# Feed-forward up projections of two transformer blocks: all 16 slabs make two products first, and five products each in a second pass

## The chip, the cores and the metric

The kernel runs on one core of a Trainium2 chip. Its time is the device time of one execution in microseconds (us), as the median of the executions shown. The profile is of one execution, which has its own time and its own span (first to last instruction). PE is the engine of matrix products, DVE and POOL are the two that add and subtract whole tiles, ACT copies, casts and applies Relu and Square, SP only issues DMAs. ACT and POOL issue DMAs as well. Each engine has its own list of instructions and runs it strictly in order; between engines they wait on semaphores.

## The reference, cut to what matters

Two transformer blocks follow each other on one sequence of 1024 tokens of width 1024, in float32. Each ends in a feed-forward layer with a hidden width of 4096:

```
h = rms_norm(x, ffn_pre_norm)
f = square(relu(h @ w_up)) @ w_down
x = x + rms_norm(f, ffn_post_norm)

h2 = modulate(rms_norm_2(x, g_pre_mlp), sh2, sc2)
ff = square(relu(h2 @ w_mlp_in)) @ w_mlp_out
x  = x + gt2 * rms_norm_2(ff, g_post_mlp)
```

The change lies in `h @ w_up` and `h2 @ w_mlp_in`. The second block also needs `mod = c @ w_ada + b_ada`, six rows of 1024; the first two are made beside the first block's up projection.

## The kernel before, in words

Every float32 operand is split in two parts (hi and lo), and a product is three matmuls: hi by hi, hi by lo, lo by hi (`mm3`, L169). The up projection saves multiplications by a scheme of Strassen's kind: tokens and the width of the model are halved, so that `h` has four quarters, and instead of eight quarter products a slab of 256 hidden columns takes seven, on sums of quarters. A product has 12 matmuls of 128 by 512 columns (four steps of the width, three matmuls each), so a slab of seven has 84, and one stage with 16 slabs has 1344. The four quarters of the first half of the tokens (`b11` and `b21`, hi and lo) are the tiles `hq`, those for the other five products (`b22`, `t1` to `t4`) the tiles `hq_t`.

The stage (`up_stage`) runs twice, once in each block. First the output projection of the attention goes over two halves of the tokens. The epilogue of the second half (norm, transposes, `hq_t`) takes long, so PE is given other work meanwhile: the two products of 12 slabs that need `hq` alone (`LEAD`, L1032 and L1141 to L1151). Weights for it come a pair of slabs at a time through `load_w`, with one raw buffer `w_raw` and two buffers each of `w_hi` and `w_lo`. Their results are copied out of PSUM by ACT (L1150) into one of two staging tiles with one buffer each, and stored to `fx_dr` by a DMA on ACT (L1151). Then `slab` (L1060) goes over all 16 slabs: it loads the whole 256 columns of weights again (L1065; raw buffers `w_raw` and `fraw` in turn), DVE makes four sums of weight quarters in `fws` (L1073), ACT casts each part to hi (L1079) and copies it to PSUM (L1081), DVE subtracts for lo (L1082). The first two parts lie in one pair of `w_hi` and `w_lo`, the other three in the second pair, so a slab takes all the buffers there are. PE makes five products for slabs 0 to 11 (loading the two stored ones back, L1098) and seven for slabs 12 to 15. Each product has one of six PSUM buffers. DVE adds the products up (L1105 to L1132), in tiles `fx`, `fu2`, `fu3`, `f11`, `f00`; ACT applies Relu and Square (L1050, L1051). Last, POOL makes five more sums of the four results for the down projection (L1137) in tiles `fs` and stores each by a DMA of its own (L1043); ACT stores the other two. `fu2`, `fu3`, `f11` and `fws` have one buffer each, `fs` two.

In block 1, `side(c)` adds a step of `modulation` after each slab: DVE multiplies rows of `w_ada` by a column (L1245, L1247) out of 512 KB tiles.

Which instruction stands where in each engine's list is set by a scheduler at build time from its own estimates; `tc.high_priority` lets the lead products go ahead. After the stage, `ffn_down` begins with weights that POOL subtracts (L1180).

Of the kernel before, what the change touches and what calls it, by code (L numbers as in the profile page):

```python
# [65 lines left out]
def tile_two_blocks(ctx: ExitStack, tc: tile.TileContext, I, out):  # L66
# [965 lines left out]
    LEAD = 12  # L1032

    def lead_w(w_up, c):

        return load_w([w_up[:, 256 * (c + i):256 * (c + i) + P].rearrange("(k p) n -> p k n", p=P) for i in range(2)],
                      16, P)

    def ffn_up(hq, w_up, fl, fp, first, side):
# [13 lines left out]
        def p1(pool, a11):  # L1053
            acc = mm_tile()
            product(acc, a11, "b11")
            x = pool.tile([P, 512], F32, name="fx")
            ACT.copy(x, acc)
            return x

        def slab(c, lead):  # L1060
# [16 lines left out]
            def halves_of(t, n, v):  # L1077

                ACT.copy(t[0][:, n], v)  # L1079
                pt = tr_tile().rearrange("p (k n) -> p k n", k=4)  # L1080
                ACT.copy(pt, r32(t[0][:, n]))  # L1081
                DVE.tensor_tensor(out=t[1][:, n], in0=v, in1=pt, op=ALU.subtract)  # L1082

            def op(t, n):
                return [x[:, n] for x in t]
# [4 lines left out]
            halves_of(u[0], 0, s2)  # L1090
            halves_of(u[0], 1, s3)
            halves_of(u[1], 0, s1)
            halves_of(u[1], 2, a22)
            halves_of(u[1], 1, s4)
            if lead:
                x, f11 = (fp.tile([P, 512], F32, name=nm) for nm in ("fx", "f00"))
                for i, t in enumerate((x, f11)):
                    SP.dma_start(t, fx_dr[:, 512 * (2 * c + i):512 * (2 * c + i) + 512])  # L1098
                q2 = f11
            else:  # L1100
# [5 lines left out]
            if not lead:
                q2 = mm_tile()
                product(q2, op(u[0], 3), "b21")
                f11 = fp.tile([P, 512], F32, name="f00")
# [542 lines left out]
```

## Time and profile before

| | us |
|---|---|
| median of 3 executions (lowest, highest) | 2893.92 (2881.35, 2893.98) |
| the profiled execution | 2892.09 |
| its span | 2890.4 |
| PE busy in the span | 2659.9 (92%) |
| DVE, ACT, POOL busy | 1898.6, 1404.9, 833.3 |

The profiled execution's own time is 1.7 us more than its span, which is what lies around the program. Busy times of PE hide short pauses and a slow clock, because matmuls overlap in the pipeline; a stage is read from the starts of its first and last matmul, and from the row that says what each pause waited for. The granted clock of PE stands as a share of its full speed: 1.00 is 2.4 GHz and 0.5 is 1.2 GHz.

### The profile page before, as it was taken

The numbers are of one execution on the slowest core, as the hardware profiler recorded it, in microseconds if no ns is written. First come the engines' busy times: TensorE is split into PE (matmuls) and PEld (weight loads), VectorE is DVE, ScalarE is ACT, GpSimd is POOL, SyncE is SP. The second block draws the span as 40 slices with busy tenths as digits, with TensorE's granted clock in tenths as the row PEclk, the third lists the DMA queues.
The fourth block names the chain that finished last, engine by engine and source line by source line (L and its number), as shares of the span: only waits on it lengthen the run. The fifth ranks groups of instructions, "written<-read, shape, count | busy, mean of one in ns | idle before, by whom it ended". The sixth has DMA issues, their size and how long they took to land.

```text
span 2890.4 us, 39700 instructions
## 1 busy us (share of the span) xinstructions
PE 2659.9 (92%) x13801; PEld 2242.6 (78%) x13801; DVE 1898.6 (66%) x3526; ACT 1404.9 (49%) x2608; POOL 833.3 (29%) x840
## 2 busy tenths in 40 slices
PE   8999999999777889999999999989999778989996
PEld 7788889998656668877887788877897666778785
DVE  7668799768656655577745368785477555545665
ACT  4544666455545644354511256563278445543342
POOL 1242344200244451434100022112200444552413
PEclk9999999999898999999999999999999898999998
DMA  3386585357556467777654554436656454387785
GB/s 127 94 286 195 157 235 159 109 170 246 188 192 207 155 245 244 269 255 250 212 180 164 189 166 139 121 106 204 211 183 227 159 175 160 139 296 240 257 282 191
DMA packets 377406, 562.24 MB, mean 195 GB/s; under 512 B 39427, under 2 KB 215658, under 8 KB 377206
## 3 DMA queue, kind: packets, MB, share of 16 engines
q1 hardware_dynamic: 348278, 488.39, 52.3%
q0 software_dynamic: 12800, 41.95, 3.6%
q10 hardware_dynamic: 16128, 29.37, 2.7%
q8 instruction: 109, 1.79, 0.3%
q14 instruction: 91, 0.75, 0.1%
HBM read 408.83 MB, written 150.78 MB: 194 GB/s over the span
## 4 chain that ended last, share of the span: by engine, by line
PE 22%; DMA 13%; DVE 8%; ACT 5%; POOL 4%; issue 4%; SPq 0%; POOLq 0%; ACTq 0%; DVEq 0%
PE mm L173 19%; DMA dwr<-in_w_mlp_out 3%; DMA fs<-fs 3%; DVE w_lo L179 2%; POOL fs L1137 2%; POOL dwr L1180 1%; PE po L906 1%; DVE w_lo L209 1%; PE tr L898 1%; ACT w_hi L178 1%; DMA w_raw<-in_w_mlp_out 1%; DMA mixR<-mrg 1%; POOL w_raw L1180 1%; DMA m_sg<-sig 1%; ACT w_hi L203 1%
## 5 line engine op out<-in xcount | busy, mean ns | idle before, releaser
L173 PE MATMUL mm<-w_hi,df 128*128 128x512 f32 x1792 | 560.6, 393 | 20.8 <-ACT w_hi L178 13.5
L173 PE MATMUL mm<-hq_t,w_hi 128*128 128x512 f32 x1280 | 415.9, 408 | 114.1 <-DVE fu L1105 103.2
L173 PEld LDWEIGHTS mm<-w_hi,df 128*128 128x128 f32 x1792 | 338.9, 189 | 96.6 <-ACT w_hi L178 14.8
L173 PEld LDWEIGHTS mm<-hq_t,w_hi 128*128 128x128 f32 x1280 | 251.5, 198 | 179.0 <-DVE fu L1105 65.4
L173 PE MATMUL mm<-w_lo,df 128*128 128x512 f32 x896 | 352.7, 394 | 10.0 <-DVE w_lo L179 9.9
L173 PE MATMUL mm<-h_hi,w_hi 128*128 128x512 f32 x736 | 290.9, 395 | 0.0
L173 PE MATMUL mm<-h_lo,w_hi 128*128 128x512 f32 x736 | 289.4, 393 | 0.0
L173 PE MATMUL mm<-h_hi,w_lo 128*128 128x512 f32 x736 | 289.0, 393 | 0.0
L173 PE MATMUL mm<-hq_t,w_lo 128*128 128x512 f32 x640 | 256.6, 404 | 1.4 <-DVE w_lo L1082 1.4
L209 DVE TENSOR_TENSOR w_lo<-w_raw,w_hi 128x1024 fp32r<-128x1024 f32 (+1 forms) x138 | 172.8, 1276 | 101.6 <-ACT w_hi L203 101.1
L203 ACT CAST w_hi<-w_raw 128x1024 fp32r<-128x1024 f32 (+1 forms) x138 | 138.8, 1048 | 165.2 <-PE mm L173 57.6
L179 DVE TENSOR_TENSOR df<-dfr,df 128x1024 fp32r<-128x1024 f32 x112 | 160.3, 1445 | 87.1 <-ACT df L178 86.9
L173 PEld LDWEIGHTS mm<-w_lo,df 128*128 128x128 f32 x896 | 169.7, 189 | 49.9 <-DVE w_lo L179 15.4
L1180 POOL TENSOR_TENSOR dwr<-dwr 128x1024 f32<-128x1024 f32 x40 | 99.5, 2488 | 317.7 <-DMA dwr<-in_w_mlp_out 183.9
L173 PE MATMUL mm<-w_hi,mixT 128*128 128x256 f32 x1024 | 184.9, 282 | 5.8 <-DVE m_sg L1448 2.8
L1137 POOL TENSOR_TENSOR fs<-f,f 128x512 f32<-128x512 f32 x32 | 43.9, 1372 | 469.1 <-ACT f L1051 459.7
L1082 DVE TENSOR_TENSOR w_lo<-fws,tr 128x512 fp32r<-128x512 f32 x128 | 85.6, 685 | 140.5 <-ACT tr L1081 139.6
L179 DVE TENSOR_TENSOR w_lo<-dwr,w_hi 128x1024 fp32r<-128x1024 f32 x56 | 104.6, 1869 | 101.4 <-ACT w_hi L178 101.0
L178 ACT CAST df<-dfr 128x1024 fp32r<-128x1024 f32 x112 | 115.6, 1050 | 108.8 <-PE mm L173 75.6
L173 PEld LDWEIGHTS mm<-h_hi,w_hi 128*128 128x128 f32 x736 | 138.3, 188 | 33.8 <-issue 2.8
L173 PEld LDWEIGHTS mm<-w_hi,mixT 128*128 128x128 f32 x1024 | 157.6, 189 | 7.8 <-ACT w_hi L203 5.1
L1137 POOL TENSOR_TENSOR fs<-fu,f 128x512 f32<-128x512 f32 x96 | 129.6, 1352 | 114.0 <-DMA fs<-fs 110.3
(418 smaller groups left out, 6306.8 us busy)
## 6 DMA issues: line engine op xcount, KB each, us to landing
dfr<-fs SPq DMA_DIRECT2D x112, 512.0 KB, 6.3
fs<-fs POOLq DMA_DIRECT2D x160, 256.0 KB, 2.6
w_raw<-in_w_in SPq DMA_DIRECT2D x32, 1024.0 KB, 4.9
ada_raw<-in_w_ada SPq DMA_DIRECT2D x48, 512.0 KB, 4.3
w_raw<-in_w_down SPq DMA_DIRECT2D x48, 512.0 KB, 4.1
dwr<-in_w_down SPq DMA_DIRECT2D x48, 512.0 KB, 5.4
w_raw<-in_w_mlp_out SPq DMA_DIRECT2D x48, 512.0 KB, 6.2
dwr<-in_w_mlp_out SPq DMA_DIRECT2D x48, 512.0 KB, 4.6
```

What stands on the lines that cost most here:

```text
L173: PE.matmul(ps, l, r, start=first and n == 0, stop=final and n == last)
L178: ACT.copy(hi, src)
L179: DVE.tensor_tensor(out=lo, in0=src, in1=r32(hi), op=ALU.subtract)
L203: ins = ACT.copy(wh[:, step * i:step * i + step], raw[:, step * i:step * i + step])
L209: DVE.tensor_tensor(out=wl[:, c], in0=raw[:, c], in1=r32(wh[:, c]), op=ALU.subtract)
L898: PE.transpose(pt[:, 256 * j + P * i:256 * j + P * i + P], prob[i][:, ks], ident)
L906: PE.matmul(po[:, d:], vb if j else va, t[:, 256 * j:256 * j + 256 - d], start=n == 0 and m == 0, stop=n == len(groups) - 1 and m == 3)
L1082: DVE.tensor_tensor(out=t[1][:, n], in0=v, in1=pt, op=ALU.subtract)
L1137: POOL.tensor_tensor(out=t, in0=x, in1=z, op=o)
L1180: POOL.tensor_tensor(out=a, in0=a, in1=b, op=ALU.subtract if sub else ALU.add)
```

## The change

All 16 slabs go through the first pass (two products each), and the second loop makes five products for every slab; the seven-product form is gone. So `fx_dr` holds 16 slabs instead of 12. Since nothing reads `hq` after the first pass, its four tiles get new uses: `hq0` is the raw buffer of odd slabs (in place of `fraw`), `hq1` and `hq2` hold the weight sums in turn (in place of the one `fws`, which slab 0 still uses), and `hq3` takes the rows of `w_ada`, 1 MB a load instead of 512 KB, with the next load issued ahead. With the space saved, `fu2`, `fu3` and `f11` get two buffers each and `fs` seven.

```diff
-    "fp": "fws fraw fx*2 f00*2 fu2 fu3 f11 fs*2 ada_acc ada_raw*2",
+    "fp": "fws fx*2 f00*2 fu2*2 fu3*2 f11*2 fs*7 ada_acc",
...
-    fx_dr = scratch("fx_dr", (P, 2 * 12 * 512))
+    fx_dr = scratch("fx_dr", (P, 2 * 16 * 512))
...
+            self.b = [[self.tile(2 * g + i, [P, 4, 512], F32R) for i in range(2)] for g in range(2)]
+        def tile(self, i, shape, dtype):
+            return self.pool.tile(shape, dtype, name=f"hq{i}")
...
+        with tc.high_priority(offset=100):
+            for c in range(NC):
+                if c % 2 == 0:
+                    w = first if c == 0 else even_w(w_up, c)
+                for i, b in enumerate(("b11", "b21")):
+                    acc = product([t[:, 8 * (c % 2) + 4 * i:8 * (c % 2) + 4 * i + 4] for t in w], b)
+                    x = fl.tile([P, 512], F32, name=("fx", "f00")[i])
+                    ACT.copy(x, acc)
+                    ACT.dma_start(fx_dr[:, 512 * (2 * c + i):512 * (2 * c + i) + 512], x)
+        for c in range(NC):
             if c % 2:
-                raw = fp.tile([P, 2048], F32, name="fraw")
+                raw = hq.tile(0, [P, 2048], F32)
...
-            ws = fp.tile([P, 4, 4, P], F32, name="fws")
+            ws = fp.tile([P, 4, 4, P], F32, name="fws") if c == 0 else hq.tile(1 + c % 2, [P, 4, 4, P], F32)
...
-            if not lead:
-                halves_of(u[0], 2, a11)
-                halves_of(u[0], 3, a12)
...
-                x = p1(fp, op(u[0], 2))
...
+            w6, w7, w5, w4, w3 = [parts(*a) for a in ((0, 0, s2), (0, 1, s3), (1, 0, s1), (1, 1, a22), (1, 2, s4))]
...
-        for c in range(LEAD):
...
-        for c in range(NC):
-            slab(c, c < LEAD)
...
-                g = modulation(fp, 0, 2)
+                g = modulation(fp, 0, 2, lambda: hq.tile(3, [P, 4, 512], F32), 4)
```

The order of the instructions outside the two stages and the first products of the down projections is as it was. Three places differ as follows.

POOL's list in block 1, the sums of one slab from the first to its last store, in the kernel before (`fs` are the sums, `fs0` to `fs6` their places in memory):

```order
L1137 TENSOR_TENSOR fs_10025<-f00_9934,f11_9984 128x512
L1043 DMA fs0_99<-fs_10025 128x512
L1137 TENSOR_TENSOR fs_10022<-f00_9934,fu3_9969 128x512
L1043 DMA fs4_103<-fs_10022 128x512
L1137 TENSOR_TENSOR fs_10031<-fu2_9950,f11_9984 128x512
L1043 DMA fs1_100<-fs_10031 128x512
L1137 TENSOR_TENSOR fs_10028<-fu3_9969,f11_9984 128x512
L1043 DMA fs6_105<-fs_10028 128x512
L1137 TENSOR_TENSOR fs_10034<-fu2_9950,f00_9934 128x512
L1043 DMA fs5_104<-fs_10034 128x512
```

The same slab's work in the changed kernel:

```order
L1124 TENSOR_TENSOR fs_10179<-f00_10062,f11_10141 128x512
L1124 TENSOR_TENSOR fs_10182<-f00_10062,fu3_10126 128x512
L1124 TENSOR_TENSOR fs_10185<-fu3_10126,f11_10141 128x512
L1046 DMA fs0_99<-fs_10179 128x512
L1046 DMA fs4_103<-fs_10182 128x512
L1046 DMA fs6_105<-fs_10185 128x512
L1124 TENSOR_TENSOR fs_10188<-fu2_10107,f11_10141 128x512
L1124 TENSOR_TENSOR fs_10191<-fu2_10107,f00_10062 128x512
L1046 DMA fs1_100<-fs_10188 128x512
L1046 DMA fs5_104<-fs_10191 128x512
```

A store no longer stands between every two sums, and the two sums that read `fu2` are the last.

DVE's list in block 1, a stretch of the second loop in the kernel before (`fu2_10373` and `fu3_10392` are one slab's, `f00_10496` the next slab's):

```order
L1105 TENSOR_TENSOR fu2_10373<-fx_10356,mm_10360 128x512
L1082 TENSOR_TENSOR w_lo_10474<-fws_10466,tr_10484 128x512
L1116 TENSOR_TENSOR fu3_10392<-fu2_10373,mm_10379 128x512
L1082 TENSOR_TENSOR w_lo_10474<-w_raw_10464,tr_10488 128x512
L1110 TENSOR_TENSOR f00_10496<-fx_10495,f00_10496 128x512
L1120 TENSOR_TENSOR f11_10407<-fu3_10392,mm_10394 128x512
L1129 TENSOR_TENSOR fu2_10373<-fu2_10373,mm_10394 128x512
L1082 TENSOR_TENSOR w_lo_10474<-fws_10466,tr_10492 128x512
L1126 TENSOR_TENSOR fu3_10392<-fu3_10392,mm_10412 128x512
L1132 TENSOR_TENSOR fu2_10373<-fu2_10373,mm_10429 128x512
```

The corresponding stretch in the changed kernel (`fu2_10246` and `fu3_10265` are one slab's, `f00_10338` and `fu2_10383` the next slab's, `hq2_10480` the sums for the slab after that):

```order
L1109 TENSOR_TENSOR f11_10280<-fu3_10265,mm_10267 128x512
L1111 TENSOR_TENSOR fu2_10246<-fu2_10246,mm_10267 128x512
L1084 TENSOR_TENSOR hq2_10480<-hq0_10474 128x512 x2
L1084 TENSOR_TENSOR hq2_10480<-hq2_10480,hq0_10474 128x512
L1116 TENSOR_TENSOR fu3_10265<-fu3_10265,mm_10286 128x512
L1084 TENSOR_TENSOR hq2_10480<-hq0_10474,hq2_10480 128x512
L1101 TENSOR_TENSOR f00_10338<-fx_10337,f00_10338 128x512
L1119 TENSOR_TENSOR fu2_10246<-fu2_10246,mm_10302 128x512
L1100 TENSOR_TENSOR fu2_10383<-fx_10337,mm_10370 128x512
L1094 TENSOR_TENSOR w_lo_10349<-hq1_10341,tr_10359 128x512
L1094 TENSOR_TENSOR w_lo_10349<-w_raw_10335,tr_10363 128x512
```

The next slab's sum of the two stored products (`f00`) stands ahead of the last sum of the slab before it (`fu2`, L1119), and the weight sums are made a slab earlier.

PE's list in block 1, the boundary of the two passes in the kernel before (`hq10`, `hq11` are the quarters of the first pass, `mm_9658` is slab 0's first product of the second loop):

```order
L173 MATMUL mm_9607<-hq11_7681,w_hi_9551 128x512
L173 MATMUL mm_9607<-hq10_7680,w_lo_9552 128x512
L173 MATMUL mm_9658<-hq_t0_8912,w_hi_9630 128x512
L173 MATMUL mm_9677<-hq_t0_8912,w_hi_9630 128x512
L173 MATMUL mm_9658<-hq_t1_8913,w_hi_9630 128x512
```

In the changed kernel (`mm_9736`, `mm_9752` are products of the first pass, `mm_9819` and `mm_9838` slab 0's first two of the second):

```order
L173 MATMUL mm_9736<-hq2_7680,w_lo_9713 128x512
L173 MATMUL mm_9819<-hq_t0_8912,w_hi_9795 128x512
L173 MATMUL mm_9819<-hq_t1_8913,w_hi_9795 128x512
L173 MATMUL mm_9736<-hq2_7680,w_hi_9712 128x512
L173 MATMUL mm_9736<-hq3_7681,w_hi_9712 128x512
L173 MATMUL mm_9736<-hq2_7680,w_lo_9713 128x512
L173 MATMUL mm_9838<-hq_t0_8912,w_hi_9795 128x512
L173 MATMUL mm_9838<-hq_t1_8913,w_hi_9795 128x512
L173 MATMUL mm_9752<-hq0_7678,w_hi_9712 128x512
```

Slab 0's first two products now begin with 27 matmuls of the first pass still behind them, and 20 of those come after both.

## Rows read from the trace of the kernel before

**Rows 1.** The page's costliest groups: instruction, count, busy, mean ns, idle before
```profile
L173 PE MATMUL mm<-hq_t,w_hi 128*128 128x512 f32 x1280 | 415.9, 408 | 114.1 <-DVE fu L1105 103.2
L1137 POOL TENSOR_TENSOR fs<-fu,f 128x512 f32<-128x512 f32 x96 | 129.6, 1352 | 114.0 <-DMA fs<-fs 110.3
```

**Rows 2.** Busy time by stretch, with matmul counts, granted clock, DMA share, GB/s
```profile
core 0: us, PE busy (x) PEld busy (x) DVE busy (x) ACT busy (x) POOL busy (x), PEclk, DMA share, GB/s
654.20:1044.10 389.90, 330.11 (x1384) 264.91 (x1383) 253.57 (x406) 214.08 (x374) 143.40 (x149) 0.92 0.57 196
2155.50:2540.40 384.90, 325.32 (x1377) 262.76 (x1377) 226.42 (x370) 223.65 (x403) 142.67 (x149) 0.93 0.52 178
2233.00:2273.00 40.00, 40.00 (x178) 33.12 (x177) 27.94 (x41) 25.09 (x48) 15.20 (x16) 1.00 0.53 172
2273.00:2457.00 184.00, 135.10 (x543) 107.87 (x541) 92.86 (x147) 89.96 (x167) 82.90 (x90) 0.88 0.48 165
1040.00:1080.00 40.00, 31.15 (x120) 22.55 (x120) 22.91 (x17) 15.76 (x19) 26.59 (x21) 0.87 0.79 275
2520.00:2560.00 40.00, 31.31 (x125) 24.42 (x124) 19.75 (x23) 19.20 (x28) 23.67 (x19) 0.87 0.83 307
```

**Rows 3.** PE in order of time: start, duration, instruction, idle before it
```profile
816.63 1.02 PE L1255 MATMUL mm<-ada_acc,cst 128*1 128x512 f32 x2
831.32 1.19 PE L173 MATMUL mm<-hq_t,w_hi 128*128 128x512 f32 x2 [13.67 <-DVE fu L1105]
...
2272.68 0.62 PE L173 MATMUL mm<-hq_t,w_hi 128*128 128x512 f32 x2
2273.14 0.39 PE L173 MATMUL mm<-hq_t,w_lo 128*128 128x512 f32 x1
2283.07 1.22 PE L173 MATMUL mm<-hq_t,w_hi 128*128 128x512 f32 x2 [9.55 <-DVE fu L1105]
...
2539.20 0.62 PE L173 MATMUL mm<-hq_t,w_hi 128*128 128x512 f32 x2
2539.89 0.62 PE L173 MATMUL mm<-hq_t,w_hi 128*128 128x512 f32 x2
```

**Rows 4.** POOL in order of time, one stall in block 2
```profile
2338.72 1.26 POOL L1137 TENSOR_TENSOR fs<-fu,f 128x512 f32<-128x512 f32 x1 [1.26 <-DMA fs<-fs]
2340.27 0.56 POOL L1043 DMA_DIRECT2D fs<-fs  x1 [0.30 <-POOL fs L1137]
2344.48 1.25 POOL L1137 TENSOR_TENSOR fs<-fu,f 128x512 f32<-128x512 f32 x1 [3.65 <-DMA fs<-fs]
```

**Rows 5.** DVE in order of time, beside the same stall
```profile
2339.28 1.84 DVE L1073 TENSOR_TENSOR fws<-fraw 128x512 f32<-128x512 f32 x2
2345.77 0.69 DVE L1105 TENSOR_TENSOR fu<-fx,mm 128x512 f32<-128x512 f32 x1 [3.31 <-POOL fs L1137]
```

**Rows 6.** Groups by shape between 2240 and 2480 us, columns as in rows 1
```profile
L1081 ACT COPY tr<-w_hi 128x512 f32<-128x512 f32 x62 | 34.8, 580 | 2.1 <-DVE w_lo L1082 2.1
L1043 POOL DMA_DIRECT2D fs<-fs x59 | 32.8, 556 | 16.5 <-POOL fs L1137 13.1 <-issue 2.9 <-DMA fs<-fs 0.6
L1082 DVE TENSOR_TENSOR w_lo<-fws,tr 128x512 fp32r<-128x512 f32 x48 | 32.2, 685 | 77.1 <-ACT tr L1081 76.8
L1079 ACT CAST w_hi<-fws 128x512 fp32r<-128x512 f32 x48 | 29.2, 615 | 39.1 <-PE mm L173 33.7 <-DVE fws L1073 5.4
L1050 ACT ACTIVATE fu<-fu 128x512 f32<-128x512 f32 x24 | 14.5, 622 | 0.4 <-ACT f L1051 0.4
L1073 DVE TENSOR_TENSOR fws<-fraw 128x512 f32<-128x512 f32 x12 | 10.2, 888 | 0.2
L1073 DVE TENSOR_TENSOR fws<-w_raw 128x512 f32<-128x512 f32 x12 | 9.1, 778 | 0.1
```

**Rows 7.** Landing times of the loads from `fx_dr` (L1098)
```profile
DMA to landing us min/median/max: 3.4/4.5/5.7
```

**Rows 8.** PE at the end of the first pass in block 1
```profile
722.98 0.39 PE L173 MATMUL mm<-hq,w_lo 128*128 128x512 f32 x1
728.83 1.22 PE L173 MATMUL mm<-hq_t,w_hi 128*128 128x512 f32 x2 [5.47 <-ACT hq_t L356]
```

**Rows 9.** SP: slab 0's weights issued; then DVE: their sums; then ACT: the last copy out
```profile
706.90 0.38 SPq L1065 DMA_DIRECT2D w_raw<-in_w_up  x1
...
715.34 1.29 DVE L1073 TENSOR_TENSOR fws<-w_raw 128x512 f32<-128x512 f32 x2 [1.42 <-DMA w_raw<-in_w_up]
...
731.77 0.57 ACT L1150 COPY f<-mm 128x512 f32<-128x512 f32 x1
```

**Rows 10.** PE at the start of the two down projections
```profile
1055.97 0.79 PE L173 MATMUL mm<-w_hi,df 128*128 128x512 f32 x1 [5.40 <-ACT w_hi L178]
2551.60 0.80 PE L173 MATMUL mm<-w_hi,df 128*128 128x512 f32 x1 [7.70 <-ACT w_hi L178]
```

More of the change, by code (lines that the diff above doesn't have):

```diff
@@ L1040, in ffn_up, with left, product @@
         NC = w_up.shape[1] // 256
-        def left(c, i, t, q=SP):
+        def left(c, i, t, q):
             q.dma_start(fs_dr[i][:, 512 * c:512 * c + 512], t)
-        def product(acc, w, b, first=True, final=True):
+        def product(w, b):
+            acc = mm_tile()
             hi, lo = hq.operand(b)
-            mm3(acc, [(w[0][:, k], w[1][:, k], hi[:, k], lo[:, k]) for k in range(4)], first=first, final=final)
+            mm3(acc, [(w[0][:, k], w[1][:, k], hi[:, k], lo[:, k]) for k in range(4)])
+            return acc
         def square(f):
@@ L1075, in slab, with parts @@
                   for nm in ("w_hi", "w_lo")] for _ in range(2)]
-            def halves_of(t, n, v):
-                ACT.copy(t[0][:, n], v)
+            def parts(i, n, v):
+                hi, lo = (t[:, n] for t in u[i])
+                ACT.copy(hi, v)
                 pt = tr_tile().rearrange("p (k n) -> p k n", k=4)
[L1081 to L1085, printed above, removed]
@@ L1087, in slab @@
-            if not lead:
-                halves_of(u[0], 2, a11)
-                halves_of(u[0], 3, a12)
[L1090 to L1100, printed above, removed]
-                x = p1(fp, op(u[0], 2))
@@ L1102, in slab @@
-            q6 = mm_tile()
-            product(q6, op(u[0], 0), "t2")
+                ACT.copy(pt, r32(hi))
+                DVE.tensor_tensor(out=lo, in0=v, in1=pt, op=ALU.subtract)
+                return hi, lo
+            w6, w7, w5, w4, w3 = [parts(*a) for a in ((0, 0, s2), (0, 1, s3), (1, 0, s1), (1, 1, a22), (1, 2, s4))]
+            q6 = product(w6, "t2")
             u2 = fp.tile([P, 512], F32, name="fu2")
             DVE.tensor_tensor(out=u2, in0=x, in1=q6, op=ALU.add)
[L1106 to L1109, printed above, removed]
@@ L1127, in slab @@
             square(f12)
[L1128 to L1131 removed]
+            q3 = product(w3, "b22")
             DVE.tensor_tensor(out=f21, in0=f21, in1=q3, op=ALU.add)
             square(f21)
[L1134 removed]
+            for i, y, z, o in ((0, f11, f22, ALU.add), (4, f11, f12, ALU.add), (6, f12, f22, ALU.subtract),
                                (1, f21, f22, ALU.add), (5, f21, f11, ALU.subtract)):
                 t = fp.tile([P, 512], F32, name="fs")
[L1137 removed]
+                POOL.tensor_tensor(out=t, in0=y, in1=z, op=o)
                 left(c, i, t, POOL)
[L1141 to L1153 removed]
             side(c)
@@ L1282, in modulation @@
                 modulation_sum(i - 1, acc, pool)
-            acc = yield from modulation_acc(i, pool)
+            acc = pool.tile([P, 512], F32, name="ada_acc")
+            for k in range(8):
+                r = raw[:, k % m, :]
+                if k == 0:
+                    DVE.tensor_scalar(acc, r, col(R_C), None, ALU.mult)
+                else:
+                    DVE.scalar_tensor_tensor(out=acc, in0=r, scalar=col(R_C + k), in1=acc, op0=ALU.mult, op1=ALU.add)
+                if k % m == m - 1:
+                    raw = load(n * i + k // m + 1)
+                if k % 2:
+                    yield
         modulation_sum(2 * m1 - 1, acc, pool)
         modulation_columns(pool, m0, m1)
-        yield
     def gated_gain(dst, tmp, m, g):
```

86 lines of the change are left out of this document (29 added, 57 removed).

## The prediction, as it was put on record before the changed kernel ran

> **What bounds the kernel now.** I read the page's costliest groups first. PE's largest idle time stands before the matmuls of the five products, 114 us, and 103 of it ended with DVE's `fu` addition L1105 [rows 1]. Then the busy times by stretch [rows 2]: the up projections take 389.9 us in block 1 and 384.9 us in block 2, PE is idle for 60 us in each, and its granted clock is 0.92 and 0.93, so it spends part of them at the lower of its two levels.
>
> What a stage would take without pauses: three matmuls start 0.69 us apart [rows 3], and 178 fit in 40.0 us [rows 2], so 0.227 us each. 1344 of them are 305 us. The 40 others of block 1 (transposes, modulation) add about 5, the 33 of block 2 about 4. So 310 and 309 us; the stages lose **80 and 76 us**, 60 idle and the rest at the lower clock (0.5 in the stretches after pauses of 9.55 or 13.67 us [rows 3]).
>
> Who makes PE wait is read in the order of time. PE stops until DVE's L1105; DVE sat idle before it until POOL had finished a sum [rows 5]; POOL sat 1.26 and 3.65 us before its sums until its own stores had landed [rows 4]. All 32 `fu` additions of the slabs write the single `fu2`, which POOL's last two sums of the slab before still read, and POOL has two `fs` buffers, so every other sum waits for a DMA to land. In sum 110 of POOL's 114 us of idle time before these sums are such landings [rows 1]. DVE's list is in order, so behind L1105 stand the subtractions for `w_lo` and the additions that empty PSUM, and with six PSUM buffers PE soon stops.
>
> One stretch shows a second loop without this. Between 2233 and 2273 us, the first three slabs of block 2 with five products, POOL has not yet fallen behind, and PE is busy for all of 40.0 us at clock 1.00 [rows 2]. The next 184 us, of the same work, hold only 543 matmuls, 0.339 us each.
>
> **The change part by part.**
>
> Buffers. With two `fu2`, `fu3`, `f11`, the addition for slab c waits for POOL's sums of slab c-2; with seven `fs`, POOL doesn't wait for landings. POOL's own work in a slab is five sums of 1.35 us, five issues of 0.56 and up to five waits of 0.30 for its own sum [rows 1, 4, 6]: 11.0 us. PE needs 60 matmuls, 13.6 us. So POOL stays ahead, and the wait goes rather than moves.
>
> What is late next? ACT has five parts of 0.62 + 0.58 us and eight activations of 0.62 [rows 6], 11.0 us, with two DMA issues still under 13.6. DVE has 4 weight sums, 5 subtractions and 7 additions, 16 times 0.685 = 11.0 us, and in block 1 two of modulation, 12.3. All are below PE but not far, and they wait for each other. Bounds for what a slab loses: nothing (the stretch at 2233), and the 6.7 us that it loses today (0.339 less 0.227, times 60). I take 0.5 us, near the stretch that has this work, times 15 slabs: **7 us per stage** kept.
>
> The weights' buffers. `w_hi` and `w_lo` are as many as before, so parts 1 and 2 of the next slab are made while PE has three products left (8.2 us), parts 3 to 5 while it has the first two (5.4 us). The stretch at 2233 ran so without a pause.
>
> Boundary of the passes. Before, slab 0's raw weights were issued at 706.90, the sums began at 715.34 [rows 9], and PE's last matmul of the lead ended at 723.4 [rows 8]. In the new order PE needs slab 0's `w_hi` with 27 matmuls still to do, 6.1 us earlier. Issue to the first `w_hi`: 8.4 + three sums 2.0 + cast 0.6 = 11.0 us, against 723.2 - 706.9 - 6.1 = 10.2: 1 us late. Then parts 3 to 5 need the buffer of the last lead pair, which is free only when PE has nothing else to do: a cast behind another, a copy, a subtraction, 3 us. Slab 1 can't be loaded into `hq0` until the last `b11` product is read, but 12 matmuls of `b21` and slab 0's last 36 with that wait cover 13.7 us against 8.4 + 2.0 + 1.9. I take **6 us per stage** with some of the lower clock. The nearest row for more is the 5.47 us of today's boundary [rows 8]; it waited for the epilogue's `hq_t`, and four more slabs of first pass (96 matmuls, 21.8 us) now cover that.
>
> First pass of 16 slabs. Its results leave through staging tiles of one buffer each. After 12 slabs ACT's last copy starts at 731.77 [rows 9], 8.6 us behind PE, so it loses 0.7 us a slab; after 16 it is 11.4 us behind, less than five free PSUM buffers (5 products of 2.72, 13.6 us). Cost nothing; bound, if ACT falls behind twice as fast, 9 us per stage. The added DMA (2 MB of weights, 4 MB to and from `fx_dr` per stage) lies beside PE.
>
> DMA rate. A slab moves 1 MB raw, 0.5 MB of stored products and 1.75 MB of results: 3.4 million bytes in 13.6 us, 250 GB/s, and 289 with modulation. The trace has 307 GB/s at a share of 0.83 [rows 2]. It fits, but landings will lengthen.
>
> Start of the down projections. PE pauses 5.40 and 7.70 us there today [rows 10], at a granted clock of 0.87 [rows 2], waiting for weights that go through DMA, POOL and ACT. The stage will end with less of POOL's and DMA's work done, so I add **3 us** per stage (between 0 and another 7).
>
> Sum: block 1 gains 80 - 7 - 6 - 3 = 64, block 2 gains 76 - 16 = 60. 2892.1 - 124 = 2768 us for the execution that was profiled; the median lies 1.8 above it: **2770 us**.
>
> **A rule that speaks against it.** DVE's weight sums, which have two inputs in SBUF, took 0.89 and 0.78 us on average in the two forms that come first, against 0.685 for subtractions that read PSUM, and two of them 1.84 us while POOL's sum of 2338.72 ran [rows 4 to 6]. The two forms take turns by slab, so that is 0.41 and 0.19 us, 0.3 us per slab on average at today's spacing. The Trainium skill (SBUF — State Buffer, section "SBUF: two separate sides") says that a DVE instruction with two SBUF inputs and a GpSimd instruction that reads SBUF share a port pair which the first to start holds for its whole length. The trace agrees in kind. By rule alone nothing says how often they meet; if always, the sum would be that of the first rival, and by the row it is 0.3 us, inside the 0.5 us above.
>
> **Rivals.**
>
> 1. DVE becomes the bound through POOL. POOL's sums fill 6.8 of 13.6 us instead of 6.8 of 20. Five DVE instructions of a slab have two SBUF inputs (four weight sums and `f00`), seven in block 1. If half of them wait a whole sum of 1.3 us, DVE needs 11.0 + 3.3 = 14.3 us in block 2 and 12.3 + 4.6 = 16.9 in block 1: 15 slabs times 0.7 and 3.3, 60 us, time 2830. If all wait, 17.5 and 21.4 us: 175 us, time 2945, **slower** than today. It decides from 4.1 us a slab on (124 us over 30 slabs). For it: the means in rows 6. Against: only the first two of four sums are longer at all, and DVE is busy for 28 us of 40 where PE runs full [rows 2].
>
> 2. `f00` becomes the ring. It keeps two buffers, and POOL's last sum of a slab frees one. Then the load (issue 0.3, landing 3.4 to 5.7 [rows 7]), DVE's `f00` sum 0.7, which the new order puts ahead of the slab's last `fu2` sum, six ACT steps until that is squared (3.7), and two sums of POOL (2.6): 10.7 to 13.0 us against 13.6. At a landing of 8 us under the higher DMA rate the slab takes 15.3, 30 slabs lose 51 us, time about 2820. Against: it needs a landing beyond any in the trace.
>
> 3. The change doesn't do what it says: POOL stays the limit, with one wait exchanged for another. It would need sums of 1.9 us instead of 1.35 for POOL to reach even 13.8 us; to keep today's 20.3 us, sums of 3.2. Time about 2890.
>
> **Chances.** The forecast, 2745 to 2797, 0.70. Rival 1 at its half and rival 2, 2797 to 2860, together 0.21. Rival 3, 0.03; rival 1 in full, slower, 0.04. Below 2745 (no loss at boundary and start, nothing per slab) 0.02. The range is 2748 to 2825: it takes in most of the two middle cases. What a measurement of this kernel can tell from no change is about 0.5%, 14 us: faster 0.93, same 0.03, slower 0.04.
>
> **What the new profile would show.** Right: no idle time of PE before `hq_t` matmuls put to the `fu` addition; POOL's sums no longer waiting for `fs` landings; the second pass of either block at 13.6 to 14.5 us a slab and a granted clock of 1.00; stages of about 325 us. Wrong: PE waiting for `w_lo` in every slab with DVE busy above 12.5 us of it and weight sums of 1.2 us and more (rival 1); DVE's `f00` sum waiting for its load, or ACT's Relu for it (rival 2); POOL busy throughout (rival 3). A pause of over 10 us between the passes would say that I underrated the boundary, one of over 15 us at the down projections that the backlog was only moved there.

## The result, and the profile after

The changed kernel takes **2820.99 us** (median of 4 runs, 2817.31 to 2821.78); the kernel before ran at 2889.98 beside it. The ratio is 0.9763, 95% interval 0.9735 to 0.979: 69 us faster. The forecast was 2770, with a range of 2748 to 2825. So the sign and the range held, the range by 4 us, but only 69 of the 124 us arrived: the time lies outside the 2745 to 2797 that had a chance of 0.70, in the band above it that had 0.21.

Busy time by stretch in the changed kernel: the up projections of blocks 1 and 2, then their down projections (columns as in [rows 2]).

```profile
656.80:1012.70 355.90, 326.06 (x1386) 257.51 (x1385) 273.38 (x406) 207.14 (x367) 147.48 (x152) 0.98 0.68 230
2127.60:2477.40 349.80, 320.96 (x1379) 255.95 (x1378) 231.40 (x369) 219.30 (x396) 143.81 (x152) 0.98 0.62 212
1012.70:1349.00 336.30, 320.15 (x1379) 259.97 (x1378) 208.73 (x225) 144.83 (x183) 124.96 (x60) 0.97 0.74 256
2477.40:2798.50 321.10, 310.52 (x1346) 254.17 (x1344) 197.62 (x189) 128.04 (x143) 113.61 (x49) 0.98 0.77 264
```

The up projections went from 389.9 and 384.9 us to 355.9 and 349.8; I had expected 323 and 322. All of the shortfall is in these two rows. The granted clock rose from 0.92 and 0.93 to 0.98, and what is left is mostly waiting: of the 46 and 41 us beyond the 310 and 309 without pauses, PE is idle for 30 and 29.

The page's costliest groups, after:

```profile
L173 PE MATMUL mm<-hq_t,w_hi 128*128 128x512 f32 x1280 | 397.2, 399 | 16.8 <-ACT w_hi L1091 10.0
L173 PE MATMUL mm<-hq_t,w_lo 128*128 128x512 f32 x640 | 247.5, 402 | 41.3 <-DVE w_lo L1094 41.3
```

The 103 us that PE lost to the `fu` addition [rows 1] are all but gone. PE now waits for `w_lo`, 41.3 us, and in block 2 that comes in nearly every slab (twelve times, 16.4 us). Why DVE is late there is read from DVE's waits between 2240 and 2440 us (in total, times, longest):

```profile
DVE w_lo L1094 <- ACT tr L1093: 30.1, 38, 1.4
DVE hq L1084 <- DMA hq<-in_w_mlp_in: 20.5, 6, 5.4
DVE hq L1084 <- DMA w_raw<-in_w_mlp_in: 17.9, 6, 4.2
```

Twelve slabs, twelve waits for raw weights, 38.4 us: 3.2 us a slab. DVE's list over one slab shows how that closes into a loop:

```profile
2411.07 0.69 DVE L1084 TENSOR_TENSOR hq<-hq 128x512 f32<-128x512 f32 x1 [2.90 <-DMA hq<-in_w_mlp_in]
2411.68 0.68 DVE L1109 TENSOR_TENSOR f<-fu,mm 128x512 f32<-128x512 f32 x1
...
2415.79 0.68 DVE L1084 TENSOR_TENSOR hq<-hq,hq 128x512 f32<-128x512 f32 x1
...
2418.55 0.69 DVE L1094 TENSOR_TENSOR w_lo<-hq,tr 128x512 fp32r<-128x512 f32 x1 [0.88 <-ACT tr L1093]
2419.15 0.68 DVE L1094 TENSOR_TENSOR w_lo<-w_raw,tr 128x512 fp32r<-128x512 f32 x1
...
2427.34 0.69 DVE L1084 TENSOR_TENSOR hq<-w_raw 128x512 f32<-128x512 f32 x1 [3.34 <-DMA w_raw<-in_w_mlp_in]
```

and SP's list beside it:

```profile
2404.05 0.38 SPq L1073 DMA_DIRECT2D hq<-in_w_mlp_in  x1
...
2419.86 0.38 SPq L1073 DMA_DIRECT2D w_raw<-in_w_mlp_in  x1
```

The last reader of a raw buffer is the fourth `w_lo` of its slab (2419.15, it reads `w_raw`). 0.03 us after it, SP issues the reload, and the first sum that needs it starts 7.48 us later. That sum belongs to the slab after next, yet DVE's list has it *ahead* of the fourth `w_lo` of the next slab, which frees the other buffer. So a slab goes: reload 7.0 us (issue 2404.05 to first sum 2411.07), then from first sum to fourth `w_lo` 8.8 us; together 15.8 us (issue 2404.05 to issue 2419.86), while PE needs 13.6. Over 13 reloads of block 2 the time from issue to first sum was 5.5 to 9.5 us, 7.0 at the median.

### The profile page after: what moved, and what is told of

It is laid out like the page before. It is cut to its first block, busy times and chain, and to the rows that moved or that the text cites. A ratio compares the mean times of both kernels' runs of the same rounds, so it can differ in the third digit from the quotient of the medians.

```text
span 2819.8 us, 39665 instructions
## 1 busy us (share of the span) xinstructions
PE 2657.0 (94%) x13801; PEld 2235.4 (79%) x13801; DVE 1923.9 (68%) x3518; ACT 1395.6 (49%) x2592; POOL 830.8 (29%) x840
## 4 chain that ended last, share of the span: by engine, by line
PE 45%; DMA 22%; DVE 15%; ACT 7%; issue 6%; POOL 5%; SPq 1%; DVEq 0%; POOLq 0%; ACTq 0%
PE mm L173 34%; DMA w_raw<-in_w_down 2%; POOL w_raw L1152 2%; PE po L909 2%; DVE w_lo L179 2%; DMA w_raw<-in_w_mlp_out 2%; DMA hq<-in_w_up 2%; DMA f<-fx_dr 2%; DMA w_raw<-in_w_mlp_in 2%; DVE w_lo L209 2%; DMA hq<-in_w_mlp_in 2%; PE tr L901 2%; DMA dwr<-in_w_down 1%; ACT w_hi L1091 1%; DVE hq L1084 1%
## 5 line engine op out<-in xcount | busy, mean ns | idle before, releaser
L173 PE MATMUL mm<-hq_t,w_hi 128*128 128x512 f32 x1280 | 397.2, 399 | 16.8 <-ACT w_hi L1091 10.0
L173 PEld LDWEIGHTS mm<-hq_t,w_hi 128*128 128x128 f32 x1280 | 242.1, 192 | 79.0 <-ACT w_hi L1091 26.7
L173 PE MATMUL mm<-hq_t,w_lo 128*128 128x512 f32 x640 | 247.5, 402 | 41.3 <-DVE w_lo L1094 41.3
L209 DVE TENSOR_TENSOR w_lo<-w_raw,w_hi 128x1024 fp32r<-128x1024 f32 (+1 forms) x146 | 183.4, 1280 | 102.1 <-ACT w_hi L203 100.8
L203 ACT CAST w_hi<-w_raw 128x1024 fp32r<-128x1024 f32 (+1 forms) x146 | 146.8, 1049 | 163.7 <-PE mm L173 59.8
L179 DVE TENSOR_TENSOR df<-dfr,df 128x1024 fp32r<-128x1024 f32 x112 | 167.8, 1510 | 87.8 <-ACT df L178 83.7
L173 PEld LDWEIGHTS mm<-hq_t,w_lo 128*128 128x128 f32 x640 | 122.5, 191 | 80.4 <-DVE w_lo L1094 55.4
L173 PEld LDWEIGHTS mm<-h_hi,w_lo 128*128 128x128 f32 x736 | 138.4, 188 | 27.1
L173 PEld LDWEIGHTS mm<-h_lo,w_hi 128*128 128x128 f32 x736 | 138.4, 188 | 26.4 <-issue 0.2
```

Of the source, the lines that this page charges most:

```text
L173: PE.matmul(ps, l, r, start=first and n == 0, stop=final and n == last)
L179: DVE.tensor_tensor(out=lo, in0=src, in1=r32(hi), op=ALU.subtract)
L203: ins = ACT.copy(wh[:, step * i:step * i + step], raw[:, step * i:step * i + step])
L209: DVE.tensor_tensor(out=wl[:, c], in0=raw[:, c], in1=r32(wh[:, c]), op=ALU.subtract)
```

## The experiments

Theory A is this loop: the raw weights' reload sets the slab. Rivals: B, the order of ACT's casts and copies makes `w_lo` late wherever the weights land; P (C in the first texts), DVE's and POOL's sums hold each other up, by the rule in the prediction; F, the loop of `f00` through POOL's last sum.

Times are medians with ratios to the kernel before, run beside it; the two columns of stages are the up projections in the profiled run, where before had 389.9 and 384.9, the changed kernel 355.9 and 349.8.

| | edit | us | ratio, 95% interval | block 1 | block 2 |
|---|---|---|---|---|---|
| 1 | three raw buffers | 2797.0 | 0.9677 (0.9648 to 0.9706) | 341.9 | 338.2 |
| 2 | raw part first | 2838.8 | 0.9823 (0.9792 to 0.9853) | 361.7 | 368.9 |
| 3 | half the raw load | 2783.0 | 0.9630 (0.9603 to 0.9658) | 338.4 | 328.6 |
| 4 | two `fs` | 2835.3 | 0.9815 (0.9781 to 0.9849) | 369.8 | 344.8 |
| 5 | 1 + short POOL sums | 2750.1 | 0.9505 (0.9479 to 0.9532) | 326.6 | 314.1 |
| 6 | 1 + three `f00`, six `fs` | 2792.7 | 0.9657 (0.9633 to 0.9681) | 338.0 | 336.5 |
| 7 | before + double `fu2`, `fu3`, `f11` | 2795.6 | 0.9668 (0.9645 to 0.9690) | 352.7 | 322.5 |
| 8 | single `fu2`, `fu3`, `f11` | 2837.5 | 0.9812 (0.9786 to 0.9839) | 368.7 | 349.7 |
| 9 | one tile of weight sums | 2794.2 | 0.9657 (0.9631 to 0.9683) | 342.7 | 324.5 |
| 10 | 9 + `w_raw` free early | 2791.7 | 0.9670 (0.9648 to 0.9693) | 343.2 | 325.0 |
| 11 | 10 + three `f00`, six `fs` | 2799.6 | 0.9705 (0.9682 to 0.9729) | 341.5 | 324.4 |
| 12 | short POOL sums alone | 2780.9 | 0.9600 (0.9566 to 0.9634) | 347.3 | 328.3 |

**1, a third raw buffer.**

```diff
-            if c % 2:
+            if c % 3 == 1:
                 raw = hq.tile(0, [P, 2048], F32)
+            elif c % 3 == 2:
+                raw = fp.tile([P, 2048], F32, name="fws")
             else:
```

> A third buffer for the raw weights of the second pass (the idle fws tile takes every third slab). Theory A, the ring of the raw weights: in the changed kernel a raw buffer is freed by the fourth w_lo of slab c, the load for slab c+2 is issued 0.03 us later, lands 7.0 to 7.5 us on, and DVE, whose list has that slab's first sum ahead of the fourth w_lo of slab c+1, waits 2.9 to 3.3 us for it; so a slab of block 2 takes 7.4 + 8.6 = 15.8 us instead of 13.6. With a third buffer the load has a whole slab more: DVE's waits for raw weights go from 72 us over both blocks to under 15, the 1.9 us steps at the first product of the second group go, a slab takes 13.6 to 14.2 us, and the time falls by 30 to 50 us, to 2770 to 2790 (ratio to before 0.96). Theory B, the order of ACT and DVE: three casts, a Relu and a Square stand between the third cast and its copy, so PE waits 1.5 us for w_lo in every slab wherever the weights land; time falls by at most 10 us. Theory C, the port that DVE and POOL share: no change beyond 5 us, DVE's sums get longer.

25 us faster than the changed kernel by the ratios, and between 2240 and 2440 us DVE no longer waits for raw weights at all. So the reload was on the path. But the time misses A's 2770 to 2790, and a slab still takes 15.1 us. What came instead is in DVE's groups between 2240 and 2440 us of this kernel (mean ns behind the comma):

```profile
L1096 DVE TENSOR_TENSOR w_lo<-hq,tr 128x512 fp32r<-128x512 f32 x58 | 39.1, 680 | 28.4 <-ACT tr L1095 28.4
L1103 DVE TENSOR_TENSOR f<-fx,f 128x512 f32<-128x512 f32 x14 | 16.9, 1210 | 8.5 <-issue 5.6 <-POOL fs L1126 1.8 <-DMA f<-fx_dr 1.1
L1086 DVE TENSOR_TENSOR hq<-fws 128x512 f32<-128x512 f32 x8 | 12.7, 1629 | 0.1
L1086 DVE TENSOR_TENSOR hq<-w_raw 128x512 f32<-128x512 f32 x8 | 12.6, 1617 | 0.1
L1086 DVE TENSOR_TENSOR hq<-hq 128x512 f32<-128x512 f32 x8 | 12.4, 1588 | 0.1
```

DVE's first two weight sums of a slab more than doubled and the `f00` sum nearly did; the slab's other two sums and the subtraction that reads PSUM stayed at 0.68. The overlap itself, DVE's row and then POOL's:

```profile
2341.53 3.55 DVE L1086 TENSOR_TENSOR hq<-hq 128x512 f32<-128x512 f32 x2
```

```profile
2341.38 2.54 POOL L1126 TENSOR_TENSOR fs<-fu,f 128x512 f32<-128x512 f32 x2
```

Now that the weights are there early, DVE's first two sums fall upon POOL's last two. The excess is (1.61 - 0.685) * 2 + (1.21 - 0.685) = 2.4 us a slab. In the changed kernel, where DVE stood waiting until POOL was done, it was 0.65 (between the same times twelve `f00` sums of 1.10 and twelve each of 0.81, 0.75 and 0.72).

**2, the raw part first.**

```diff
-            w6, w7, w5, w4, w3 = [parts(*a) for a in ((0, 0, s2), (0, 1, s3), (1, 0, s1), (1, 1, a22), (1, 2, s4))]
+            w4, w6, w7, w5, w3 = [parts(*a) for a in ((0, 0, a22), (0, 1, s2), (1, 0, s3), (1, 1, s1), (1, 2, s4))]
+            q4 = product(w4, "t4")
...
-            q4 = product(w4, "t4")
```

> The part made from the raw weights themselves (a22) is made first instead of fourth, with its product first; buffers as in the changed kernel. Theory A: the raw buffer is free about 6 to 8 us earlier, so its reload lands before DVE asks for it; slabs of 13.6 to 14.2 us, time 2770 to 2795. Theory B: nothing in ACT's casts and copies gets shorter, time within 10 us of the changed kernel's 2821. Theory C: no change beyond 5 us.

Slower than the changed kernel, which no theory had. The waits for raw weights all but went, but the edit also reordered the rest: the `f00` sum now stands last, behind `f21`. DVE's waits in the same stretch:

```profile
DVE f L1102 <- issue: 33.6, 8, 4.8
DVE f L1102 <- DMA f<-fx_dr: 9.7, 2, 5.9
```

That is the `f00` loop of my second rival, in a kernel that I had not made for it: POOL's last sum of a slab ends at 2310.34, SP issues the `f00` load at 2312.0, and DVE, idle for 4.45 us, starts its sum at 2320.30. The run says nothing on the size of the reload.

**3, half the raw load.**

```diff
-            SP.dma_start(raw.rearrange("p (k n) -> p k n", k=8),
-                         w_up[:, 256 * c:256 * c + 256].rearrange("(k p) n -> p k n", p=P))
+            SP.dma_start(raw.rearrange("p (k n) -> p k n", k=8)[:, 0:4],
+                         w_up[0:512, 256 * c:256 * c + 256].rearrange("(k p) n -> p k n", p=P))
...
-            (a11, a21), (a12, a22) = ([r4[:, h, i] for i in range(2)] for h in range(2))
+            (a11, a21), (a12, a22) = ([r4[:, 0, i] for i in range(2)] for h in range(2))
```

> The second pass loads only the first 512 of the 1024 rows of each slab's raw weights, 0.5 MB instead of 1, and the sums read that half twice; instructions, waits and buffers are otherwise those of the changed kernel. Theory A: the landing falls from 7.2 us to about 4, which is more than the 2.9 to 3.3 us that DVE waits for it, so a slab falls to 13.6 to 14.2 us and the time to 2770 to 2795. Theories B and C: the load is not on the path, the time stays within 10 us of 2821.

2783, as theory A said: no instruction or buffer changed, only the bytes of the reload, and 38 us went. The kernel leaves out half of the weights. (DVE still waits 27 us for raw weights in block 2, so the loop is shorter here, not gone.)

**4 and 8, the two halves of the buffer change undone.**

```diff
-    "fp": "fws fx*2 f00*2 fu2*2 fu3*2 f11*2 fs*7 ada_acc",
+    "fp": "fws fx*2 f00*2 fu2*2 fu3*2 f11*2 fs*2 ada_acc",     (4)
+    "fp": "fws fx*2 f00*2 fu2 fu3 f11 fs*7 ada_acc",           (8)
```

> The changed kernel with two fs buffers instead of seven, all else kept. If the stores' landings were what slowed POOL and through it all else (my reading of the trace before, without the single fu2), POOL waits again for landings of 3 to 5 us before three of five sums, a slab of POOL takes 11 + 3 * 2 to 3.5 = 17 to 21 us, and the time rises by 30 us or more towards 2870 to 2890. If the single fu2, fu3 and f11 alone were to blame, POOL's lag is absorbed by the second buffers and the time stays within 10 us of 2821.

> The changed kernel with a single fu2, fu3 and f11, seven fs kept. If the single fu2 was the bound, DVE's first addition of a slab waits again for POOL's last sums of the slab before, which in the changed kernel end 4 to 5 us after it (POOL's last sum 2408.4, the addition 2401.2): 4 to 7 us a slab over 30 slabs, time 2900 or more. If the landings through two fs were the bound, POOL now runs without them and the time stays within 20 us of 2821.

Each costs about 15 us, though their intervals just touch that of the changed kernel (0.9781 and 0.9786 against 0.979). 4 lies between its two readings, 8 in the band that denied the single `fu2`. But of the up projections only block 1's got longer, by 14 and 13 us. In block 2 they stay at 344.8 and 349.7, with DVE waiting 39.6 and 39.7 us for raw weights: there the reload sets the slab, and neither kind of buffer can show what it is worth beyond that. Still, 8 keeps the single tiles and its block 2 is 35 us below the kernel before: seven `fs` and the new order, which the run doesn't tell apart, also open the loop that bounded it. What the second tiles do by themselves needed 7.

**7, the buffers alone, in the kernel before.**

```diff
-    "fp": "fws fraw fx*2 f00*2 fu2 fu3 f11 fs*2 ada_acc ada_raw*2",
+    "fp": "fws fraw fx*2 f00*2 fu2*2 fu3*2 f11*2 fs*2 ada_acc ada_raw",
...
```

The lines left out make the modulation load 0.25 MB at a time into its one buffer.

> The kernel before with two buffers for fu2, fu3 and f11 (fs stays at two) and nothing else of the change; to make room, the modulation of block 1 has one buffer of 0.25 MB instead of two of 0.5, so block 2, which has no modulation, is what to read. If the single fu2 was what bounded the kernel before, as I predicted, block 2's up projections fall from 384.9 us to 345 to 360, and DVE's idle time before the fu addition that ended with POOL's sums goes. If the stores through two fs buffers were the limit, POOL still waits for landings, and they stay above 370.

Block 2, the last row here, falls from 384.9 to 322.5 us, beyond what was expected, and the whole kernel beats the changed one:

```profile
653.70:1006.40 352.70, 327.40 (x1385) 261.24 (x1384) 267.79 (x411) 213.70 (x373) 140.02 (x145) 0.96 0.64 215
2123.70:2446.20 322.50, 315.75 (x1378) 258.43 (x1377) 234.09 (x376) 228.11 (x405) 145.58 (x152) 0.98 0.63 214
```

So second buffers for `fu2`, `fu3`, `f11` are enough to open the loop of the kernel before; two `fs` suffice. By 8, that loop needed the single tiles and also a late POOL, late by its stores' landings or by its old order; the kernel before with seven `fs` alone would tell, and was not run. The rest of the change *cost* 27 us in block 2; 9 shows which part.

**9, one tile of weight sums.**

```diff
-            ws = fp.tile([P, 4, 4, P], F32, name="fws") if c == 0 else hq.tile(1 + c % 2, [P, 4, 4, P], F32)
+            ws = fp.tile([P, 4, 4, P], F32, name="fws")
```

> The changed kernel with one tile for the weight sums (fws for every slab) instead of two (hq1 and hq2 in turns); raw weights keep two buffers. Theory A2, the look-ahead: because the sums have two tiles, DVE's list has the sums of slab c+1 ahead of the fourth w_lo of slab c, which is what frees the raw buffer, so the reload (7.4 us) stands in the loop of every slab; with one tile the sums come behind that w_lo, the raw weights have a whole slab to land, and block 2's up projections fall from 349.4 us to 320 to 332, as the seventh experiment's 322.2, which also has one tile; time 2765 to 2785. Theory P, the port: DVE's weight sums still meet POOL's sums as in the first experiment, 335 to 342 us a stage, time 2790 to 2800. Rival: the second tile was needed, since the sums of a slab must now wait until the last w_lo of the slab before; then stages over 350 us, time 2825 or more.

This is the test of what put the reload on the path. Taking a buffer *away* saves 25 us in block 2. DVE's list and SP's now read:

```profile
2328.91 0.69 DVE L1094 TENSOR_TENSOR w_lo<-w_raw,tr 128x512 fp32r<-128x512 f32 x1 [0.35 <-ACT tr L1093]
...
2331.68 2.17 DVE L1084 TENSOR_TENSOR fws<-hq 128x512 f32<-128x512 f32 x2
...
2345.75 2.17 DVE L1084 TENSOR_TENSOR fws<-w_raw 128x512 f32<-128x512 f32 x2
```

```profile
2329.63 0.38 SPq L1073 DMA_DIRECT2D w_raw<-in_w_mlp_in  x1
```

The sums of the next slab (2331.68) come behind the fourth `w_lo`; the reload issued at 2329.63 is wanted at 2345.75, 16.1 us later, and between 2240 and 2440 us DVE never waits for raw weights. A slab takes 14.1 us. Two things kept the time at 2794, above the 2765 to 2785 expected: block 1 stays at 342.7, and the down projections take 340.6 and 334.3 us, 4 and 13 more than in the changed kernel. PE stands at their start:

```profile
1005.27 2.08 PE L173 MATMUL mm<-w_hi,df 128*128 128x512 f32 x4 [5.74 <-ACT w_hi L178]
...
2443.41 2.07 PE L173 MATMUL mm<-w_hi,df 128*128 128x512 f32 x4 [7.62 <-ACT w_hi L178]
```

**10 and 11, after that pause and `f00` again; and 6.** 10 is 9 with the raw weights from slab 1 on in `hq0` and `hq1`; 6 and 11 are 1 and 10 with other counts.

```diff
-            if c % 2:
-                raw = hq.tile(0, [P, 2048], F32)
+            if c:
+                raw = hq.tile(1 - c % 2, [P, 2048], F32)      (10, 11)
-    "fp": "... f00*2 ... fs*7 ada_acc",
+    "fp": "... f00*3 ... fs*6 ada_acc",                       (6, 11)
```

> The ninth experiment's kernel (one tile of weight sums), with the raw weights of slabs 1 to 15 in hq1 and hq0 in turns, so that w_raw is free for the down projections' first block from slab 1 on. In the ninth kernel PE stands 6.3 and 8.0 us at the start of the down projections, because their weights come through w_raw and dwr late. If w_raw's late release is the cause, those pauses fall to under 3 us each and the time to 2783 to 2788. If dwr (the second block) or the df products' landing is the cause, they stay, and the time is within 5 us of 2794. The slabs themselves: no change, 13.6 to 14.0 us in block 2.

> The same with three f00 and six fs. Theory F, the ring of f00: in the ninth kernel DVE waited 23 us in block 2 for f00 loads (15.1 of it put to issue, 8.2 to landings) and ACT 11.9 behind it; if that is still on the path, the up projections of block 2 fall from 324 to 314 to 319 and those of block 1 from 342 to 330 to 338, time 5 to 15 us under the tenth's. Theory P, the port: what remains in block 1 is DVE's modulation beside POOL (1.11 us each against 0.75), which this doesn't touch; within 4 us of the tenth.

> Three raw buffers as in the first experiment, three f00 buffers and six fs instead of two and seven; nothing left out. Theory F, the ring of f00: the load of f00 no longer waits for POOL's last sum of slab c-2; the waits of DVE's f00 sum go (5.6 us in six slabs of block 2) and ACT's Relu of it (9.3 us in nine); time 2775 to 2788. Theory P: DVE's weight sums still take 2.8 to 3.6 us for two beside POOL, time within 8 us of 2797.

10 is within 5 us of 9 and its pauses stay (5.10 and 9.65 us), so `w_raw` isn't what they wait for. In both kernels and both blocks PE starts 0.05 to 0.06 us after ACT has cast the second block of weights, out of `dwr`. In 9's block 2 that cast follows POOL's subtraction, which stands in POOL's list behind a sum of the last slab:

```profile
2439.86 2.42 POOL L1152 TENSOR_TENSOR dwr<-dwr 128x1024 f32<-128x1024 f32 x1
2442.31 1.04 ACT L178 CAST w_hi<-dwr 128x1024 fp32r<-128x1024 f32 x1 [0.32 <-POOL dwr L1152]
```

No run moved it. A third `f00` gains nothing that can be told (6: ratio 0.9657 against 0.9677, intervals overlapping; 11: 0.9705 against 0.967). It hardly shortens the waits either: between 2200 and 2440 us DVE stands 8.5 us before `f00` sums in 1 and 6.8 in 6, 19.5 in 10 and 20.7 in 11. So the missing buffer isn't what these wait for; whether the waits cost time stays open.

**5 and 12, short POOL sums.**

```diff
-            q.dma_start(fs_dr[i][:, 512 * c:512 * c + 512], t)
+            d = fs_dr[i][:, 512 * c:512 * c + 512]
+            q.dma_start(d.rearrange("p (a n) -> p a n", a=4) if q is POOL else d, t)
...
-                t = fp.tile([P, 512], F32, name="fs")
-                POOL.tensor_tensor(out=t, in0=y, in1=z, op=o)
-                left(c, i, t, POOL)
+                t = fp.tile([P, 512], F32, name="fs")[:, :P]
+                POOL.tensor_tensor(out=t, in0=y[:, :P], in1=z[:, :P], op=o)
+                left(c, i, t.unsqueeze(1).to_broadcast([P, 4, P]), POOL)
```

> The first experiment's kernel (three raw buffers), with POOL's five sums of a slab over 128 of the 512 columns, and that quarter stored four times over; it leaves out three quarters of each sum, while the number of instructions, waits and stored bytes stay. Theory P, the port that DVE and POOL share: with three raw buffers DVE's first two weight sums run beside POOL's last two sums and take 2.8 to 3.6 us for two instead of 1.3; with short POOL sums they fall to 0.7 each, a slab of block 2 goes from 15.0 to 13.6 to 14.1 us and the time from 2797 to 2765 to 2780 (ratio to before under 0.962). Theory F, the ring of f00: POOL's last sum frees f00, its load takes 5.5 us to land, and ACT's casts stand behind the Relu of that sum; POOL then ends 2 to 3 us earlier, so about half of the same gain, but DVE's sums beside POOL would not have mattered by themselves. If neither holds, within 5 us of 2797.

> The changed kernel with POOL's five sums of a slab over 128 of the 512 columns and that quarter stored four times over, as in the fifth experiment, but with its two raw buffers; it leaves out three quarters of each sum. Theory A, the reload of the raw weights is the bound of a slab in block 2: DVE still waits about 40 us for raw weights there, block 2's up projections stay at 340 to 350 us (349.4 now), those of block 1 fall from 355.5 to 335 to 350 since DVE's modulation goes from 1.41 us each to 0.77; time 2795 to 2815. Theory P, the port bounds it in the changed kernel too, and the wait for weights only fills the gap: both stages at 313 to 328 us as in the fifth experiment, time 2750 to 2775.

With three raw buffers (5), shortening POOL's sums from 1.3 to 0.46 us brings 47 us, more than theory P said; block 2 reaches 314.1 us, 5 above the time without any pause. The same DVE groups as in 1, between 2220 and 2400 us:

```profile
L1104 DVE TENSOR_TENSOR f<-fx,f 128x512 f32<-128x512 f32 x13 | 9.9, 761 | 16.3 <-issue 8.1 <-POOL fs L1127 4.3 <-DMA f<-fx_dr 3.9
L1087 DVE TENSOR_TENSOR hq<-w_raw 128x512 f32<-128x512 f32 x8 | 5.2, 688 | 0.1
L1087 DVE TENSOR_TENSOR hq<-fws 128x512 f32<-128x512 f32 x8 | 5.2, 688 | 0.1
```

Without the overlap the sums are back at 0.69. (POOL also ends earlier, which the run doesn't tell apart from the shorter sums of DVE; 6 and 11 don't settle it, since they left DVE's waits for `f00` nearly as they were.)

Alone (12) it brings 40 us, which lies between the theories: time and block 2 fall well below A's figures, block 2 to the upper edge of P's, while block 1 lies in A's band. Its SP row and DVE row show the loop still closed, but faster:

```profile
2329.11 0.38 SPq L1074 DMA_DIRECT2D w_raw<-in_w_mlp_in  x1
...
2343.56 0.38 SPq L1074 DMA_DIRECT2D hq<-in_w_mlp_in  x1
```

```profile
2334.50 0.69 DVE L1085 TENSOR_TENSOR hq<-w_raw 128x512 f32<-128x512 f32 x1 [1.26 <-DMA w_raw<-in_w_mlp_in]
```

A slab is 14.45 us: 9.1 from first sum to issue, much as in the changed kernel, but the reload takes 5.4 us here, and 5.5 at the median of 12 (5.3 to 8.2) where the changed kernel had 7.0. The same bytes move; the stores are cut in smaller pieces and the sums end sooner. Which of these lets the load land earlier was not tried apart.

## Why the prediction was right in sign and off in size

**What bounds the kernel now: right.** In block 2, experiment 7 doubles only the buffers that I named, and it comes to 322.5 us. That 309 + 7 + 6 of my terms make the same is partly luck, since 7 keeps the old boundary of the passes. Two `fs` are no bound by themselves: in 7 POOL still waited 56.7 us for their landings, while PE stood 6.3 us in all in the second pass. They may have been one of two conditions (8).

**Steady loss of 0.5 us a slab: this step failed.** Block 2's slabs took 16.4 us on average where I had 14.1 (first sums 2246.70 to 2443.12, twelve slabs). I weighed engines by their sums (all under 13.6) and took the stretch at 2233 [rows 2] as the same work. It wasn't in the same order: there the sums have one tile. The DVE rows of the change section had the sums in `hq2_10480` ahead of `w_lo_10349` from `w_raw_10335`, and their text that weight sums are made a slab earlier. I counted the buffers of `w_hi` and `w_lo`, and the raw load only at the boundary (8.4 us against 13.7); at PE's pace the steady loop leaves it 13.6 - 8.8 = 4.8 us. Experiments 1, 3 and 9 open or shorten that loop in three ways, and block 2 falls by 12, 21 and 25 us.

**Boundary of the passes, 6 us per stage: too much.** PE had no pause there in block 1 and one of 2.88 us in block 2 (`w_hi` of slab 0, 2215.22). The first pass itself cost nothing, as said.

**Start of the down projections, +3 us per stage: right for block 1, not for block 2.** Those stages took 336.3 and 321.1 us, against 332.9 and 329.2 before. Where the up projections got faster (9), both have a pause, 5.74 and 7.62 us, close to the 5.40 and 7.70 of [rows 10].

**Rival 1, DVE held by POOL: half right, and I priced the term too low.** In block 1 it is one of two causes. PE's longest pause there, 7.50 us for `w_lo`, ended at 791.24; DVE in the meantime, then POOL:

```profile
783.75 1.62 DVE L1101 TENSOR_TENSOR f<-fx,f 128x512 f32<-128x512 f32 x1 [0.30 <-issue]
785.29 1.76 DVE L1256 SCALAR_TENSOR_TENSOR ada_acc<-hq,vec,ada_acc 128x512 f32<-128x512 f32 x1
786.97 0.67 DVE L1100 TENSOR_TENSOR fu<-fx,mm 128x512 f32<-128x512 f32 x1
787.57 3.03 DVE L1256 SCALAR_TENSOR_TENSOR ada_acc<-hq,vec,ada_acc 128x512 f32<-128x512 f32 x1
790.51 0.67 DVE L1094 TENSOR_TENSOR w_lo<-hq,tr 128x512 fp32r<-128x512 f32 x1
```

```profile
783.55 1.26 POOL L1124 TENSOR_TENSOR fs<-f,fu 128x512 f32<-128x512 f32 x1 [1.92 <-ACT fu L1056]
784.78 1.72 POOL L1124 TENSOR_TENSOR fs<-fu,f 128x512 f32<-128x512 f32 x1
...
787.54 2.48 POOL L1124 TENSOR_TENSOR fs<-fu,f 128x512 f32<-128x512 f32 x2
```

A step of modulation, which I had at 0.65 us, two a slab, took 1.41 in this stage (28 of them); in 5 it took 0.77. The rule of the Trainium skill (SBUF — State Buffer, section "SBUF: two separate sides") is borne out in kind, for the operation that scales and adds as well as for plain sums: DVE's row of 3.03 us lasts as long as POOL's two sums beside it and 0.6 us more, and `fu<-fx,mm`, which reads PSUM, kept its 0.67. What the row before gave, 0.3 us a slab, was a price for one spacing of the engines; it was 0.65 in block 2 of the changed kernel and 2.4 when the weights came early. The other cause in block 1 is the reload: DVE waited 26.3 us for raw weights after slab 0, and 1 and 9 took 14 and 13 us off this block, short POOL sums in 5 another 15. Rival 1's figure of 2830 is near the measured time partly by luck: in block 2 the reload came first.

**Rivals 2 and 3.** Rival 2's "about 2820" is met by luck. The `f00` load with its 8 us landing was the wrong load: the raw weights had that landing (6.7 to 9.5 us from issue to first sum in block 2, from 2272 us on). DVE waited 4.0 us for `f00` landings in block 1, none between 2240 and 2440. POOL didn't stay the limit.

## What to carry to other kernels

A second buffer for a derived tile can change the order, not only the waiting: here the work that fills it moved ahead in its engine's list, and everything that this work reads was then wanted a step earlier. Before costing such a change, follow each load in the steady loop from its buffer's last reader to its first new reader, in the new order, and compare that span with the load's landing; here a landing of 7 us stood in a loop whose other 8.8 us left it 4.8. And do the parts of a change one by one: the three extra buffers alone were worth more than all of it, and the changed kernel without its second sum tile (2794.2 us, ratio 0.9657) beats both kernels, as three doubled buffers in the old one do (2795.6).

## What the runs showed of the hardware

- A DVE sum with two SBUF inputs beside a POOL sum of 1.3 us takes 1.6 us on average instead of 0.69, and two beside two took 3.55 (1); with one PSUM input it keeps 0.68. Two inputs of full size aren't needed: the multiplication that begins a modulation, of one SBUF tile by a column, took 0.47 us with POOL idle and 1.58 to 3.29 the three times that it met POOL's sums in block 1 of the changed kernel. With three raw buffers, shortening POOL's sums was worth 47 us of a 2797 us kernel, part of which may be that POOL ends earlier.
- The same 1 MB load took 7.0 us from issue to first use at the median in the changed kernel, and 5.5 where POOL's sums were short and its stores, of the same bytes, were in smaller pieces (12). Which of the two did it is not shown.
